# A hybrid FNet and mLSTM block in fp32: z and output gate of heads 1 to 3 as seven block products, x normalised early, u split in branch b

## The chip, the cores and the metric

The kernel runs on one core of a Trainium2 chip, in one launch. The metric is device time in microseconds (us). Before the change three runs took 775.4, 779.03 and 782.14 us; the median is 779.03. Line numbers (L88) are those of the kernel before, unless a sentence says "after".

## The reference

x is 512 positions by 1024 channels in fp32. All weights are fp32 too.

```python
h = rmsnorm(x, norm_w)
x_f, z_f, x_m, z_m, o_m, g_logits = split(h @ w_in)        # 1024, 1024, 2048, 2048, 2048, 2 x 1024 columns
y_a = (Re(fft2(x_f in 4 groups)) * silu(z_f)) @ w_fourier
x_c = silu(conv5(x_m)); q, k = block_diag(x_c); v = block_diag(x_m)
i, f gates of two directions = [q, k, v] @ w_gate + b
h_cell = mlstm(q, k, v, i, f) + flip(mlstm(flip(...)))       # 4 heads of 512 channels
h_cell = rmsnorm_per_head(h_cell * sigmoid(o_m)) * hnorm_w
y_b = ((h_cell + skip_w * x_c) * silu(z_m)) @ w_mlstm        # the bracket times silu(z_m) is u
x = x + (sigmoid(g_a) * y_a + sigmoid(g_b) * y_b) @ w_out
return rmsnorm(x, final_norm_w)
```

## The kernel before, in words

**fp32 products.** Each fp32 operand is split in two: hi, a rounded copy that ACT writes (`hi_of`, L85), and lo, the rest, that DVE subtracts (`lo_of`, L88). A product is three matmuls on TensorE (PE): hi hi, lo hi, hi lo (`mm3`, L95 to L97). The stationary tile is 128 x 128, the moving one 512 columns, or 256 in the block products.

**Weights.** They stream through `fetch` (L126, L129) on the DMA queue of SP, in units of 128 x 1024 (512 KB), into three `raw` buffers; `prepare` splits a unit into `whi` and `wlo`, `unit` hands it out. For the block products sums of weight blocks are needed: `sum_job` copies 1 MB from DRAM to DRAM on SP (L156) and adds 1 MB to it with an accumulating DMA that POOL issues (L160). One job runs at every third unit from unit 8 on, 17 in all. The accumulate of a job waits for the copy of the job before it.

**Order.** Work is written stage by stage, and a scheduler then sets the order of PE, ACT, DVE and POOL; instructions in `pin` keep the order of the text, as most weight transfers do. Each engine takes its instructions strictly in the order that results.

**Stages.** (1) x is loaded and split; its rows are squared and summed (`norm_rows`, L297): PE sums, DVE writes rc (L302), POOL takes the power -1/2 (L303). `norm_bcast` (L305) makes diagonals of rc on ACT (L308), multiplies them by a matrix of ones on PE (L310), and ACT writes rb (L311), the factor of each position. (2) 17 units of w_in give z of channel block 0 and x_m in 16 blocks (`proj`). They are made from x that is not normalised, and `evac` (L355) multiplies each by rb on DVE. Meanwhile the gate weights are folded with the block-diagonal q, k, v weights (`fold_gates`, L264: six multiplies on POOL, L273, and six reduces on DVE, L274); the convolution runs on DVE (L328) and feeds the gate matmuls. (3) Four heads. Each makes the scores (q by x_c), the decay weights, `o_unit` four times (L540: 24 matmuls of 512 columns each, x stationary) and `z_unit` four times (L366: 24 of 512, weights stationary), the denominators (L580 to L600; the reciprocal is L596), the split score weights whi and wlo in tiles phi and plo (L602 to L612), v (L618), the products pv (L633), the head norm (L634 to L640), transposes (L650) and u (L652, L653), which is split at once into tiles sa and sb. (4) Branch b: 16 units of w_mlstm times u, and beside it `block_sums` (L668), which loads x again, normalises it (L673) and makes the sums of its blocks, of which th, tl, bh and bl are the splits. (5) Sixteen `group`s: gates b, x_f, z_f, gates a. A group is a product of 2 x 2 blocks with seven block products in place of eight (Strassen-Winograd), each of 4 x 3 matmuls of 256 columns. X, Z and Y are its PSUM banks; sums in PSUM and on DVE (L725, L748, L754) put the blocks together. The Fourier stages run between them. (6) The product with w_fourier, the merge, w_out, residual and last norm.

PSUM has two kinds of banks, `acc` (4) and `wk` (4). Tiles named sa and sb, so0, so1, sz0, sz1 hold different things one after another; a tile is free when its last reader is done.

## Time and profile before

| | |
|---|---|
| median of three runs | 779.03 us (775.4 to 782.14) |
| the profiled execution | 782.93 us, of which the span of the trace is 781.0 |
| granted TensorE clock, mean | 0.995 |
| bytes moved by the DMA queues | 117.03 MB |

The profile is of one execution of its own. PE is TensorE's matmuls, PEld its weight loads, DVE VectorE, ACT ScalarE, POOL GpSimd, SP SyncE, "SPq" the DMA queue that SP fills. In a window's row each engine has its busy time and its count, then the clock, the DMA engines' busy share and GB/s. In a timeline row stand start, duration, engine, line, operation, output <- inputs, and in brackets the idle time before it and what ended that. A matmul's duration is longer than the step to the next one, as they overlap.

### The profile page before, as it was taken

Reading aid. Unit: us, or ns where it says so; the run is one execution under the profiler, and the core shown is the slowest. Engines: PE = TensorE matmul, PEld = TensorE weight load, DVE = VectorE, ACT = ScalarE, POOL = GpSimd, SP = SyncE. Lnnn points to the kernel's source line nnn. Section 1 sums busy time; section 2 is a strip of 40 time slices with the busy share of each in tenths; the row PEclk is TensorE's granted clock in tenths of the full one; section 3 lists DMA queues with packets and bytes.
Section 4 is the critical chain, followed back from the end, with each engine's and each line's share of the span. In section 5 each row is a group of like instructions: output and inputs, shape, how many; then the busy total and the mean of one; then the engine's idle time right before and its main releaser. Section 6 shows DMA issues by size and latency. Waiting matters only on the chain.

```text
span 781.0 us, 10974 instructions
## 1 busy us (share of the span) xinstructions
PE 766.3 (98%) x4182; PEld 654.9 (84%) x4182; DVE 525.0 (67%) x802; ACT 417.4 (53%) x658; POOL 67.2 (9%) x139
## 2 busy tenths in 40 slices
...
GB/s 300 235 141 209 214 179 92 28 161 138 80 189 102 167 109 162 42 174 154 197 27 162 141 257 90 105 193 217 190 161 159 121 166 192 144 144 169 172 55 55
DMA packets 39446, 117.03 MB, mean 150 GB/s; under 512 B 4577, under 2 KB 5090, under 8 KB 35298
## 3 DMA queue, kind: packets, MB, share of 16 engines
...
q14 instruction: 19, 0.16, 0.1%
HBM read 114.22 MB, written 35.65 MB: 192 GB/s over the span
## 4 chain that ended last, share of the span: by engine, by line
PE 93%; DVE 2%; DMA 2%; ACT 2%; issue 0%; SPq 0%; POOL 0%; POOLq 0%; ACTq 0%; DVEq 0%
PE acc L95 16%; PE acc L97 16%; PE acc L96 16%; PE wk L95 7%; PE wk L97 7%; PE wk L96 7%; PE acc L548 3%; PE acc L547 3%; PE acc L549 3%; PE wk L291 2%; PE acc L955 2%; PE acc L953 2%; PE acc L954 2%; PE wk L618 2%; DMA raw<-in_units_dram 2%; DVE wlo L88 1%
## 5 line engine op out<-in xcount | busy, mean ns | idle before, releaser
L88 DVE TENSOR_TENSOR wlo<-raw,whi 128x1024 fp32r<-128x1024 f32 (+1 forms) x103 | 128.4, 1249 | 84.0 <-ACT whi L85 83.9
L85 ACT ACTIVATE whi<-raw 128x1024 fp32r<-128x1024 f32 (+1 forms) x103 | 106.4, 1034 | 135.2 <-PE acc L96 98.0
L97 PE MATMUL acc<-hhi,wlo 128*128 128x512 f32 x248 | 97.3, 393 | 4.3 <-DVE wlo L88 4.3
L95 PE MATMUL acc<-hhi,whi 128*128 128x512 f32 x248 | 97.8, 397 | 0.8 <-ACT whi L85 0.8
L96 PE MATMUL acc<-hlo,whi 128*128 128x512 f32 x248 | 97.7, 394 | 0.0
L97 PEld LDWEIGHTS acc<-hhi,wlo 128*128 128x128 f32 x248 | 47.0, 190 | 15.5 <-DVE wlo L88 4.7
L95 PEld LDWEIGHTS acc<-hhi,whi 128*128 128x128 f32 x248 | 46.8, 189 | 11.6 <-ACT whi L85 1.2
L96 PEld LDWEIGHTS acc<-hlo,whi 128*128 128x128 f32 x248 | 47.0, 190 | 11.3 <-DVE hlo L199 0.7
L549 PE MATMUL acc<-whi,hlo 128*128 128x512 f32 x128 | 50.4, 394 | 0.0
L548 PE MATMUL acc<-wlo,hhi 128*128 128x512 f32 x128 | 50.4, 393 | 0.0
L96 PE MATMUL acc<-sb,whi 128*128 128x512 f32 x128 | 49.9, 391 | 0.0
L95 PE MATMUL acc<-sa,whi 128*128 128x512 f32 x128 | 49.8, 390 | 0.1
L96 PE MATMUL wk<-vlo,phi 128*128 128x512 f32 x128 | 49.8, 389 | 0.0
L95 PE MATMUL wk<-vhi,phi 128*128 128x512 f32 x128 | 49.8, 390 | 0.0
L97 PE MATMUL acc<-sa,wlo 128*128 128x512 f32 x128 | 48.6, 391 | 0.0
L97 PE MATMUL wk<-vhi,plo 128*128 128x512 f32 x128 | 48.0, 389 | 0.0
L547 PE MATMUL acc<-whi,hhi 128*128 128x512 f32 x128 | 47.7, 393 | 0.0
L328 DVE SCALAR_TENSOR_TENSOR t2k<-sa,vecs,t2k 128x511 f32<-128x511 f32 (+1 forms) x64 | 45.6, 739 | 0.0
L88 DVE TENSOR_TENSOR gwl<-raw,gwh 128x1024 fp32r<-128x1024 f32 x27 | 33.0, 1222 | 15.9 <-ACT gwh L85 15.9
L85 ACT ACTIVATE gwh<-raw 128x1024 fp32r<-128x1024 f32 x27 | 28.6, 1059 | 18.3 <-PE acc L96 8.3
L95 PEld LDWEIGHTS wk<-vhi,phi 128*128 128x128 f32 x128 | 24.0, 188 | 5.8 <-issue 0.8
L95 PEld LDWEIGHTS acc<-sa,whi 128*128 128x128 f32 x128 | 24.0, 188 | 5.4 <-ACT whi L85 0.5
...
## 6 DMA issues: line engine op xcount, KB each, us to landing
...
```

The costliest lines, as they stand in the source:

```text
L85: se.activation(dst, src, AF.Copy, scale=scale)
L88: ve.tensor_tensor(out=dst, in0=src, in1=hi.bitcast(F32), op=ALU.subtract)
L95: pin(te.matmul(acc, wh, xh, start=start, stop=False, **skip), pinned)
L96: te.matmul(acc, wh, xl, start=False, stop=False, **skip)
L97: te.matmul(acc, wl, xh, start=False, stop=stop, **skip)
L291: te.matmul(gate_ps, w_gate[j][:, i, :], r, start=p == 0 and n == 0, stop=last and n == 3)
L328: ve.scalar_tensor_tensor(out=cv[:, o], in0=src[:, s], scalar=cw[k], in1=cv[:, o], op0=ALU.mult, op1=ALU.add)
L547: te.matmul(ops[t], hv(x_hi, k)[:, ts], wh[:, ks], start=k == 0, stop=False)
L548: te.matmul(ops[t], hv(x_hi, k)[:, ts], wl[:, ks], start=False, stop=False)
L549: te.matmul(ops[t], hv(x_lo, k)[:, ts], wh[:, ks], start=False, stop=k == 7)
L618: te.matmul(vp[:, ds], xm[c0 + d][:, b * P : (b + 1) * P], vbf[:, d, :], start=True, stop=True)
L953: te.matmul(acc, m_hi[k][:, ts], wh, start=k == 0, stop=False)
```

## The change

**What it does.** (a) The z and o of heads 1 to 3 become block products of the class `Seven`. o takes 7 products of 24 matmuls of 256 columns (x parts stationary), z two groups of 7 products of 12 matmuls. Their block sums of weights join the jobs: `NB` is 7 instead of 4, 29 jobs instead of 17. Each of these heads now takes 14 units of 128 x 1024 instead of 8. Head 0 keeps the old form. (b) `scale_x` normalises x during units 3 to 5 (DVE, ACT, DVE) and writes it to DRAM; from unit 6 on `proj` uses it, and its outputs are copied by ACT instead of multiplied by rb on DVE. The block sums of x move to head 0 and read the normalised x back; the late ones go. (c) u stays in the tiles of x_c, and its split moves into branch b (`split_u`), to tiles sp0 to sp3 for the first four and to a pool "ub". (d) The fold's six multiplies run on DVE, in three steps at units 6 to 8. (e) The four acc banks become two px and two pz; a group's Z and Y use pz instead of wk. x_m of heads 2 and 3 goes through DRAM. In the heads, every third unit is split into sp tiles, and three split units instead of two are held ready.

**The early part on DVE.** Before, between the row sums and the second weight split (L302 is rc, L88 the lo of a weight unit or another split, L274 a reduce of the fold, L356 an evacuation by rb):

```order
L253 TENSOR_SCALAR m_45_215<-m_45_215 128x64
L302 TENSOR_SCALAR rc_222<-wk_301 128x4
L88 TENSOR_TENSOR wlo_289<-raw_184,whi_288 128x1024
L274 TENSOR_REDUCE sa_79_409<-sa_55_276 128x128
L274 TENSOR_REDUCE sa_79_409<-sa_56_278 128x128
L88 TENSOR_TENSOR wlo_332<-raw_187,whi_331 128x1024
L274 TENSOR_REDUCE sa_79_409<-sa_57_280 128x128
L356 TENSOR_TENSOR sz_51_248<-acc_223,rb_221 128x512
L356 TENSOR_TENSOR sa_54_275<-acc_250,rb_221 128x512
L356 TENSOR_TENSOR sa_66_330<-acc_294,rb_221 128x512
```

After, at the same place (L299 and L300 are the fold's multiply and reduce, L96 the lo, L332 is rc, L396 the evacuation, L380 `scale_x`):

```order
L96 TENSOR_TENSOR wlo_326<-raw_213,whi_325 128x1024
L300 TENSOR_REDUCE mhi_542<-tt_72_319 128x128
L299 TENSOR_TENSOR wf_74_323<-wf_74_323,vecs_127 128x512
L300 TENSOR_REDUCE mx_r_543<-wf_73_321 128x128
L96 TENSOR_TENSOR wlo_368<-raw_216,whi_367 128x1024
L332 TENSOR_SCALAR rc_251<-wk_338 128x4
L305 TENSOR_TENSOR mhi_542<-mhi_542 128x256
L300 TENSOR_REDUCE mx_r_543<-wf_74_323 128x128
L308 TENSOR_TENSOR wf_57_242<-mhi_542,wf_57_242 128x16x16
L308 TENSOR_TENSOR wf_58_243<-mx_r_543,wf_58_243 128x16x16
L396 TENSOR_TENSOR sz_65_285<-px_260,rb_250 128x512
L396 TENSOR_TENSOR sp_68_312<-pz_287,rb_250 128x512
...
L380 SCALAR_TENSOR_TENSOR vhi_6_128<-vhi_6_128,vecs_127,rb_250 128x512
```

The fold's multiplies and reduces and two weight splits stand ahead of rc, and the scaling of x stands between the evacuations and the convolution.

**The early part on SP.** Before (L262 gate weights, L156 the first copy for a sum, L126 weight units):

```order
L262 DMA sa_55_276<-in_gates_dram 128x512
L262 DMA sa_56_278<-in_gates_dram 128x512
L414 DMA gb_1259<-in_gbias_dram 64x2
L262 DMA sa_57_280<-in_gates_dram 128x512
L156 DMA sum_80<-in_blocks_dram 128x2048
L126 DMA raw_184<-in_units_dram 128x1024
L126 DMA raw_187<-in_units_dram 128x1024
L262 DMA sb_58_282<-in_gates_dram 128x512
L262 DMA sb_59_284<-in_gates_dram 128x512
L262 DMA sb_60_286<-in_gates_dram 128x512
L126 DMA raw_292<-in_units_dram 128x1024
```

After (L288 gate weights, L146 weight units, L182 the copy, L383 normalised x to DRAM):

```order
L288 DMA tt_71_317<-in_gates_dram 128x512
L288 DMA tt_72_319<-in_gates_dram 128x512
L288 DMA wf_73_321<-in_gates_dram 128x512
L146 DMA raw_213<-in_units_dram 128x1024
L146 DMA raw_216<-in_units_dram 128x1024
L288 DMA wf_74_323<-in_gates_dram 128x512
L146 DMA raw_329<-in_units_dram 128x1024
L466 DMA gb_1330<-in_gbias_dram 64x2
L182 DMA sum_83<-in_blocks_dram 128x2048
L146 DMA raw_371<-in_units_dram 128x1024
L383 DMA xn_256<-vhi_6_128 128x512
```

The copy moved behind three weight units and three more gate tiles.

**The start of branch b.** Before, on PE, the last product of the heads' z and the first of branch b (sa0 and sb0 are hi and lo of u's first block):

```order
L95 MATMUL acc_743_3652<-hhi3_17_125,whi_736_3612 128x512
L96 MATMUL acc_743_3652<-hlo3_21_129,whi_736_3612 128x512
L97 MATMUL acc_743_3652<-hhi3_17_125,wlo_737_3613 128x512
L95 MATMUL acc_776_3754<-sa0_350_1752,whi_740_3646 128x512
L96 MATMUL acc_776_3754<-sb0_351_1753,whi_740_3646 128x512
L97 MATMUL acc_776_3754<-sa0_350_1752,wlo_741_3647 128x512
L95 MATMUL acc_776_3754<-sa1_354_1764,whi_740_3646 128x512
```

After, on DVE, the end of head 3 and the first splits of u (L835 and L836 make u in the tiles of x_c, here sb12 to sb15; sp0 with an L96 row is the lo of u's first block, in tiles of two halves that ACT and DVE write):

```order
L607 SCALAR_TENSOR_TENSOR sz1_692_3715<-px_779_4236,sz1_692_3715 128x256
L835 SCALAR_TENSOR_TENSOR sb12_182_922<-wk_791_4370,vecs_5_127,sb12_182_922 128x512
L835 SCALAR_TENSOR_TENSOR sb13_188_939<-wk_792_4390,vecs_5_127,sb13_188_939 128x512
L835 SCALAR_TENSOR_TENSOR sb14_194_960<-wk_793_4397,vecs_5_127,sb14_194_960 128x512
L835 SCALAR_TENSOR_TENSOR sb15_198_979<-wk_794_4404,vecs_5_127,sb15_198_979 128x512
L836 TENSOR_TENSOR sb12_182_922<-sb12_182_922,sz0_691_3714 128x512
L836 TENSOR_TENSOR sb13_188_939<-sb13_188_939,sz0_691_3714 128x512
L836 TENSOR_TENSOR sb14_194_960<-sb14_194_960,sz1_692_3715 128x512
L96 TENSOR_TENSOR sp0_827_4450<-sb0_209_1043,sp0_827_4450 128x512
L836 TENSOR_TENSOR sb15_198_979<-sb15_198_979,sz1_692_3715 128x512
L96 TENSOR_TENSOR sp1_828_4456<-sb1_219_1095,sp1_828_4456 128x512
```

And on PE (px_779 is z's last block product, whose weights are in sp0 and sp1; pz_820 and px_821 are branch b's first two outputs):

```order
L103 MATMUL px_779_4236<-xph1_29_152,sp0_785_4287 128x256
L104 MATMUL px_779_4236<-xpl1_33_156,sp0_785_4287 128x256
L105 MATMUL px_779_4236<-xph1_29_152,sp1_786_4288 128x256
L103 MATMUL pz_820_4440<-sp0_827_4450,whi_788_4346 128x512
L103 MATMUL px_821_4441<-sp0_827_4450,whi_824_4444 128x512
L104 MATMUL pz_820_4440<-sp0_827_4450,whi_788_4346 128x512
L105 MATMUL pz_820_4440<-sp0_827_4450,wlo_789_4347 128x512
```

The splits of u's first blocks moved from head 0 to this place, behind the seven instructions that finish u in head 3, and into tiles that z's last product reads.

**The diff**, cut to what is spoken of (a late `group` is now a `Seven` in rows, with the same products in the same order):

```diff
 NRAW = 3
 NG = 16
+NB = 7
...
+SCALE_AT, NEW_AT, FOLD_AT = (3, 4, 5), 6, (6, 7, 8)
 Z_FIRST = 3
 LOW = ("ones", "mhalf", "warm", "vecs", "raw", "whi", "wlo", "consts", "rb", "rc", "rr", "ss", "fss", "gb")
...
+        if tag == "acc":
+            tag = ("px", "pz")[turns[0] % 2]
+            turns[0] += 1
+        return ps.tile([rows, cols], F32, tag=tag, name=f"{tag}_{count[0]}", bufs=4 if tag == "wk" else 2)
...
+    for b in range(3):
+        plan += [([blk(b, 0, 2 * S, name)], 8) for name in ("a11", "s1", "a12", "s2", "s4", "s3", "a22")]
+        seq = pairs_of([(b, 2 * S, 3 * S), (b, 3 * S, 4 * S)])
+        plan += [(seq[i : i + 2], 56) for i in range(0, len(seq), 2)]
...
+        tags, bufs = ("whi", "wlo"), 2
+        if N_HEAD0 <= i < N_HEADS and (i - N_HEAD0) % 3 == 2:
+            a = (0, 2, 0)[(i - N_HEAD0) // 14]
+            tags, bufs = (f"sp{a}", f"sp{a + 1}"), 1
+        elif first_pair <= i < last_pair and (i - first_pair) % 4 >= 2:
+            tags = ("gwh", "gwl")
...
         i = state["split"]
-        if i >= JOB_AT and (i - JOB_AT) % JOB_STEP == 0 and state["job"] < 17:
+        if i >= JOB_AT and (i - JOB_AT) % JOB_STEP == 0 and state["job"] < 4 * NB + 1:
             sum_job(state["job"])
             state["job"] += 1
-        while len(items) < (4 if "gw" in pools and state["split"] < last_pair else 2) and state["split"] < nplan - 8:
+        while len(items) < (4 if "gw" in pools and state["split"] < last_pair else 3 if N_HEAD0 <= state["split"] < N_HEADS else 2) and state["split"] < nplan - 8:
...
+        for n, t in enumerate(("tt4", "tt5", "tt6", "tt7", "wf2", "wf3")):
...
+        if not folds:
...
+        for half in range(2):
+            hs = slice(8 * half, 8 * half + 8)
+            g = grep[j, half]
+            w = wview(off)[:, hs].unsqueeze(2).to_broadcast([P, 8, 16, 4])
+            ve.tensor_tensor(out=g, in0=g, in1=w, op=ALU.mult)
+            ve.tensor_reduce(out=dst[:, hs, :], in_=g, axis=AX.X, op=ALU.add)
...
+        if i >= 8:
+            pin(nc.sync.dma_start(xm_out[i // 2][:, (i % 2) * S : (i % 2 + 1) * S], src))
...
+    def scale_x(k):
+        ve.scalar_tensor_tensor(out=xt[k], in0=xt[k], scalar=col(V_NW + k), in1=rb, op0=ALU.mult, op1=ALU.mult)
+        hi_of(x_hi[k], xt[k])
+        lo_of(x_lo[k], xt[k], x_hi[k])
+        pin(nc.sync.dma_start(xn_out[k % 4][:, (k // 4) * S : (k // 4 + 1) * S], xt[k]))
...
-        evac(sz[d], proj(), AF.Silu)
+        se.activation(sz[d], proj(x_hi, x_lo), AF.Silu)
...
-        acc = proj(hooks)
+        acc = proj(*((first_hi, first_lo) if n < NEW_AT else (x_hi, x_lo)), hooks)
...
+            if n >= NEW_AT:
+                se.activation(xm[i], acc, AF.Copy)
+                ready.append(i)
+            else:
+                waiting.append((i, xm[i], acc, None))
...
-        if n == FOLD_AT and not folded:
-            fold_gates()
+        if n in SCALE_AT:
+            at = SCALE_AT.index(n)
+            for k in range(3 * at, min(8, 3 * at + 3)):
+                scale_x(k)
+        if n in FOLD_AT:
+            fold_gates(FOLD_AT.index(n))
...
+    def block_sums(k):
+        xr = tl(f"sp{k % 2}", [P, 2, S])
+        nc.sync.dma_start(xr, xn_out[k].rearrange("p (a c) -> p a c", a=2))
...
+        def product(self, acc, name, first):
+            if self.rows:
+                wh, wl = block()
+                for k in range(4):
+                    ks = slice(k * P, (k + 1) * P)
+                    mm3(acc, wh[:, ks], wl[:, ks], xpart(0, name, k), xpart(1, name, k), first and k == 0, k == 3, group=False)
+                return
+            wh, wl = unit()
+            for k in range(4):
+                ks = slice(k * 256, (k + 1) * 256)
+                for t in range(2):
+                    ts = slice(t * P, (t + 1) * P)
+                    xh, xl = xpart(0, name, k)[:, ts], xpart(1, name, k)[:, ts]
+                    a = acc[:, t * 256 : (t + 1) * 256]
+                    go, end = first and k == 0 and t == 0, k == 3
+                    te.matmul(a, xh, wh[:, ks], start=go, stop=False, skip_group_check=True)
+                    te.matmul(a, xh, wl[:, ks], start=False, stop=False, skip_group_check=True)
+                    te.matmul(a, xl, wh[:, ks], start=False, stop=end, skip_group_check=True)
...
+        def p1(self):
+            self.X = self.new("px")
+            self.product(self.X, "b11", True)
+            se.activation(self.c11, self.view(self.X), AF.Copy)
+        def p5(self):
+            self.Z = self.new("pz")
+            self.product(self.Z, "t1", True)
+            se.activation(self.c22, self.view(self.Z), AF.Copy)
+        def p2(self):
+            Y = self.new("pz")
+            self.product(Y, "b21", True)
+            ve.tensor_tensor(out=self.c11, in0=self.view(Y), in1=self.c11, op=ALU.add)
...
+        def p6(self):
+            self.product(self.X, "t2", False)
+            se.activation(self.c12, self.view(self.X), AF.Copy)
...
+        def p3(self):
+            self.product(self.Z, "b22", False)
+            ve.tensor_tensor(out=self.c12, in0=self.view(self.Z), in1=self.c12, op=ALU.add)
...
+        def p7(self):
+            self.product(self.X, "t3", False)
+            ve.scalar_tensor_tensor(out=self.c22, in0=self.view(self.X), scalar=-1.0, in1=self.c22, op0=ALU.mult, op1=ALU.subtract)
...
+        def p4(self):
+            self.product(self.X, "t4", False)
+            se.activation(self.c21, self.view(self.X), self.func or AF.Copy, scale=-1.0)
...
-                bc = bank("acc")
+                bc = bank("acc" if h == 0 else "pz")
...
+        if h > 0:
+            o7 = Seven(so2[0][:, :, 0:256], so2[1][:, :, 0:256], so2[0][:, :, 256:512], so2[1][:, :, 256:512], False, None, AF.Sigmoid)
+            z7 = [seven_rows(sz[2 * n], sz[2 * n + 1], AF.Silu) for n in range(2)]
+            steps = [(o7.p1, o7.p5), (o7.p2, o7.p6), (o7.p3, o7.p7), (o7.p4,)]
...
+        if h >= 2:
+            for n in range(2):
+                both = tl(f"sp{2 * (h % 2) + n}", [P, 2, S])
+                nc.sync.dma_start(both, xm_out[2 * h + n].rearrange("p (a c) -> p a c", a=2))
+                xm[c0 + 2 * n], xm[c0 + 2 * n + 1] = both[:, 0], both[:, 1]
...
-        if h > 0:
-            z_unit(0)
+        if h == 0:
+            for k in range(4):
+                block_sums(k)
+        else:
+            for step in (z7[0].p1, z7[0].p5, z7[0].p2, z7[0].p6, z7[0].p3):
+                step()
...
+        if h > 0:
+            for step in (z7[1].p1, z7[0].p7, z7[1].p5, z7[1].p2, z7[1].p6, z7[0].p4, z7[1].p3, z7[1].p7):
+                step()
...
-            uu = t2k()
-            ve.scalar_tensor_tensor(out=uu, in0=tp, scalar=col(V_HN + c), in1=xc[c], op0=ALU.mult, op1=ALU.add)
-            ve.tensor_tensor(out=uu, in0=uu, in1=sz[d], op=ALU.mult)
-            u_hi[c] = tl(f"sa{c}", [P, S], F32R)
-            u_lo[c] = tl(f"sb{c}", [P, S], F32R)
-            hi_of(u_hi[c], uu)
-            lo_of(u_lo[c], uu, u_hi[c])
+            if h > 0 and d == 0:
+                z7[1].p4()
+            ve.scalar_tensor_tensor(out=xc[c], in0=tp, scalar=col(V_HN + c), in1=xc[c], op0=ALU.mult, op1=ALU.add)
+            ve.tensor_tensor(out=xc[c], in0=xc[c], in1=sz[d], op=ALU.mult)
...
+    def split_u(c):
+        if c < 4:
+            both = tl(f"sp{c}", [P, 2, S], F32R)
+            u_hi[c], u_lo[c] = both[:, 0], both[:, 1]
+        hi_of(u_hi[c], xc[c])
+        lo_of(u_lo[c], xc[c], u_hi[c])
...
                 j, c = (n, k) if n < 4 else (2 * (n % 2) + k // 4, 4 * (n // 2) + k % 4)
+                if c not in split:
+                    split.add(c)
+                    split_u(c)
                 ks = slice(k * P, (k + 1) * P)
                 mm3(accs[j], wh[:, ks], wl[:, ks], u_hi[c], u_lo[c], c == 0, c == 15)
```

330 lines of the change are left out of this document (166 added, 164 removed).

## The prediction

> **What bounds the kernel now.** The page's busy totals and its chain of waits come first, then single stretches.
>
> ```profile
> PE 766.3 (98%) x4182; PEld 654.9 (84%) x4182; DVE 525.0 (67%) x802; ACT 417.4 (53%) x658; POOL 67.2 (9%) x139
> PE 93%; DVE 2%; DMA 2%; ACT 2%; issue 0%; SPq 0%; POOL 0%; POOLq 0%; ACTq 0%; DVEq 0%
> 325.80:401.00 75.20, 75.20 (x357) 62.85 (x356) 50.69 (x84) 46.37 (x72) 10.57 (x20) 1.00 0.50 147
> ```
>
> TensorE is busy for 98% of the span and carries 93% of the chain. The third row is one stretch of 75.2 us, from the reciprocal of head 2 to that of head 3 (columns: PE, weight loads, DVE, ACT, POOL, clock, DMA share): PE never waits in it, DVE works 50.69 us, the DMA engines half of the time. So a product less is time less, as long as DVE and the DMAs, which the change loads more, stay under PE. The one large gap is early:
>
> ```profile
> 20.00:26.00 6.00, 6.00 (x35) 5.02 (x33) 0.80 (x2) 1.50 (x3) 2.75 (x3) 1.00 1.05 375
> 32.00:38.00 6.00, 5.24 (x16) 4.19 (x17) 6.00 (x10) 1.75 (x3) 0.00 (x0) 0.72 0.56 182
> 23.25 1.08 POOL L160 DMA_DIRECT2D sum<-in_blocks_dram  x1 [21.99 <-DMA sum<-in_blocks_dram]
> 24.17 1.36 POOL L303 TENSOR_TENSOR rc<-rc,mhalf 128x4 f32<-128x4 f32 x1
> 25.20 3.39 POOL L273 TENSOR_TENSOR sa<-sa,vecs 128x512 f32<-128x512 f32 x3
> 28.26 3.35 POOL L273 TENSOR_TENSOR sb<-sb,vecs 128x512 f32<-128x512 f32 x3
> 22.01 0.16 DVE L302 TENSOR_SCALAR rc<-wk 128x4 f32<-128x4 f32 x1 [2.05 <-PE wk L301]
> 25.36 7.35 DVE L88 TENSOR_TENSOR wlo<-raw,whi 128x1024 fp32r<-128x1024 f32 x1 [3.19 <-ACT whi L85]
> 33.82 1.21 DVE L88 TENSOR_TENSOR wlo<-raw,whi 128x1024 fp32r<-128x1024 f32 x1
> 26.89 1.13 PE L310 MATMUL wk<-sa,ones 128*128 128x512 f32 x2 [0.72 <-ACT sa L308]
> 32.76 0.58 PE L97 MATMUL acc<-hhi,wlo 128*128 128x512 f32 x1 [4.29 <-DVE wlo L88]
> 33.13 0.63 PE L95 MATMUL acc<-hhi,whi 128*128 128x512 f32 x1
> 33.56 0.63 PE L96 MATMUL acc<-hlo,whi 128*128 128x512 f32 x1
> ```
>
> A weight split (wlo) that takes 1.21 us elsewhere took 7.35 while POOL ran the six fold multiplies; PE stood 4.29 us for it. Then its matmuls start 0.43 us apart and the clock of that stretch reads 0.72: in 3.3 us (32.8 to 36.1) about 1.6 more are lost. The gap costs 0.72 + 4.29 + 1.6 = 6.6 us.
>
> **The products of heads 1 to 3.** Per head 192 matmuls of 512 columns become 336 of 256, with as many weight loads as matmuls.
>
> ```profile
> 480.00:500.00 20.00, 20.00 (x90) 16.55 (x89) 4.90 (x4) 3.38 (x4) 0.00 (x0) 1.00 0.29 93
> 540.00:560.00 20.00, 20.00 (x174) 20.00 (x173) 13.94 (x19) 12.04 (x20) 0.00 (x0) 1.00 0.63 203
> L95 PE MATMUL acc<-sa,whi 128*128 128x512 f32 x128 | 49.8, 390 | 0.1
> L95 PE MATMUL acc<-th,whi 128*128 128x256 f32 x100 | 28.1, 281 | 0.0
> ```
>
> The windows count every matmul that touches them, so the pitch is (20 + 0.39)/90 = 0.2266 us at 512 columns and (20 + 0.28)/174 = 0.1166 at 256. 192 x 0.2266 = 43.5, 336 x 0.1166 = 39.2: 4.3 less per head, **-13.0 us** for three. Bounds -12 and -14 from half a count. The margin is thin: at 43.5/336 = 0.1295 us per matmul nothing would be won, and in the second window the weight loads fill all 20 us.
>
> The Trainium skill (TensorE: Matmul & The Clock Gate, Back-to-back issue gap) speaks against such narrow products: it gives 131 ns per matmul at 512 columns and 81 at 128, on a straight line 98 at 256. By that ratio (an estimate) a head's products would take 336 x 0.098 = 32.9 instead of 192 x 0.131 = 25.2, 30% more. The two windows disagree, with 0.2266 and 0.1166 in this same program.
>
> **The early part.** The folds leave POOL, so the 7.35 us wlo goes. But two things move ahead of the norm. On SP the copy of the first sum now stands behind three weight units of 512 KB and three gate tiles of 256 KB that it preceded: 2.3 MB, at the 375 GB/s of the window from 20 us some 6.1 us. POOL's accumulate waits for that copy and the power that makes rc waits on POOL behind it, as at 23.25 and 24.17 above. So rc is done near 25.5 + 5.5 = 31. On DVE eleven fold instructions and two wlo now stand ahead of L332: 11 x 0.60 + 2 x 1.13 = 8.9 us from 20.0, where DVE ran out of work before, so about 28.9, the same date. Next late is the ones-matrix product of norm_bcast, on which PE queues unit 3:
>
> ```profile
> 25.56 1.28 ACT L308 ACTIVATE sa<-consts,rc 128x128 f32<-128x128 f32 x4 [0.23 <-POOL rc L303]
> 28.06 0.60 ACT L311 ACTIVATE rb<-wk 128x512 f32<-128x512 f32 x1 [0.27 <-PE wk L310]
> L673 DVE SCALAR_TENSOR_TENSOR xr<-xr,vecs,rb 128x512 f32<-128x512 f32 x8 | 5.9, 742 | 0.0
> ```
>
> 31 + 1.3 for the diagonals puts it at 32.4; PE, out of work at about 26.5, stands some 5 us, runs 1.6 slow, and has waited some 2 at the row sums before. Then DVE has the first evacuations, eight scalings (8 x 0.66 by the last row's shape, 0.74 less the 0.08 that neighbours overlap) and eight x splits (8 x 0.60) before the next wlo: I find two of them 1.3 and 0.7 late. 5 + 1.6 + 2 + 2 = 10.6 against 6.6: +4. If the copy lands as early as before, the gap shrinks to the 0.72 and the gain is -5; if both delays add, +6. I take **+2.5**: the order fixes the direction, the landing is the weak number. The 11 evacuations that leave DVE (11 x 0.60 = 6.6) pay for most of the other x work up to 135 us.
>
> **The heads' DVE chain.**
>
> ```profile
> L88 DVE TENSOR_TENSOR wlo<-raw,whi 128x1024 fp32r<-128x1024 f32 (+1 forms) x103 | 128.4, 1249 | 84.0 <-ACT whi L85 83.9
> L356 DVE TENSOR_TENSOR sz<-acc,rb 128x512 f32<-128x512 f32 x16 | 11.0, 686 | 10.9 <-PE acc L97 10.5
> L725 DVE SCALAR_TENSOR_TENSOR pr<-acc,p 128x256 f32<-128x256 f32 x8 | 3.3, 418 | 1.5 <-PE acc L97 1.5
> 323.07 0.69 DVE L595 TENSOR_TENSOR t2k<-t2k,phi 128x512 f32<-128x512 f32 x1
> 324.28 3.34 DVE L596 RECIPROCAL t2k<-t2k 128x512 f32<-128x512 f32 x1
> 341.18 0.82 DVE L88 TENSOR_TENSOR plo<-wf,phi 128x640 fp32r<-128x640 f32 x1
> 338.39 0.39 PE L95 MATMUL wk<-vhi,phi 128*128 128x512 f32 x1
> ```
>
> Per head, six more weight splits (14 for 8): 6 x 1.13 = 6.8. Block sums: three of 512 columns and six of 256, 3 x 0.61 + 6 x 0.34 = 3.9. Gone are four evacuations and four u splits, 8 x 0.60 = 4.8. So +5.9: about 57 us of DVE in a head of 75.2 - 4.3 = 70.9. The sum fits, but one chain decides: from the maximum (323.07) over the reciprocal to the last plo (342.0) 18.9 us, and the pv products wait at its end, PE reaching them at 338.39. Now four weight splits and about four sums fall into that chain (about 22 us), and the PE work beside it, o7's last products, v, and z7[0], lasts 20 to 21. I take 0.8 us of stall per head, **+2.5** in all; nothing is the lower bound (the rows of before show none), 4 per head the upper: **0 to +12**. Head 0's block sums (4 x 2.7 = 10.8 of DVE) lie under its 75 us of PE with 53 of DVE.
>
> **The start of branch b.** Before, u was split behind each head. Now the first u tiles sp0 and sp1 are also the weights of z7[1].p4, PE's last product ahead of branch b, and the lo of c = 0 stands on DVE behind four L835 and three L836.
>
> ```profile
> 436.08 2.06 DVE L652 SCALAR_TENSOR_TENSOR t2k<-wk,vecs,sb 128x512 f32<-128x512 f32 x3
> L653 DVE TENSOR_TENSOR t2k<-t2k,sz 128x512 f32<-128x512 f32 x16 | 10.3, 682 | 0.0
> L85 ACT ACTIVATE sa<-t2k 128x512 fp32r<-128x512 f32 x16 | 9.8, 629 | 18.7 <-DVE t2k L653 18.7
> 428.41 0.39 PE L97 MATMUL acc<-sa,wlo 128*128 128x512 f32 x1
> ```
>
> From the last transposes: 0.2 + 4 x 0.66 + 3 x 0.60 + 0.68 = 5.3 us until u_lo is there. PE has p4 (12 x 0.117 = 1.4, after 0.44 of transposes), waits 0.7 for the hi, has two products that need only it, and waits again: 5.3 - 0.44 - 1.4 - 0.45 = 3.0. Before, branch b began at 428.41 with no wait. **+3.0**; 1 if the transposes' sums run ahead of the row order, 5 if ACT's weight split stands before the hi.
>
> By the Trainium skill (TensorE: Matmul & The Clock Gate, What's actually happening) an idle window of about 3.4 us halves the clock for about as long; here 4.29 idle was followed by 0.43 us steps. By that rule a wait at this place beyond 3.4 would cost 1.7 more; 3.0 stays under it.
>
> **The rest.** The late groups lose two PSUM banks per role; an evacuation of 0.38 behind a 1.05 us split still lies under the 1.4 us of a product: **+0.5** (0 to +5). The later fnw load is covered by about 16 us of out products, at most 2 if not. x and xm through DRAM: 2 MB written, 2 MB read, no wait on the path. Branch b's DVE loses eight xr rows with their sums and gets sixteen u splits, in a stretch where PE waited 0.07: nothing.
>
> Sum: -13.0 + 2.5 + 2.5 + 3.0 + 0.5 = -4.5. The profiled execution took 782.93, so 778.4. It lies 3.9 above the median of 779.03; on that footing **774.5 us**. A measurement of this kernel tells 1% from no change: below 771.2 is faster, above 786.8 slower.
>
> **The rivals.** *Everything is covered* (0.27): the heads wait for nothing, as before, the copy lands early enough for the early part to come out even, branch b costs 1: -13.0 + 1 = -12, **767.0**. For it: 75.20 of 75.20 busy in the heads. Against: the rows on SP and POOL.
>
> *DVE takes over in the heads* (0.13): the plo chain ends 6 us after PE's cover in each of three heads, for instance when z7's sums are served before it. -4.5 + 18 - 2.5 = +11, **790**. It decides from 2.3 us per head for slower than before (7 us: 4.5 + 2.5), from 4.9 for more than 1%. For: the chain already ends 3.6 us after PE's first pv. Against: 14 us of DVE idle in each head.
>
> *The DMAs take over in the heads* (0.10):
>
> ```profile
> q1 hardware_dynamic: 3057, 13.77, 25.3%
> q0 software_dynamic: 864, 6.29, 22.2%
> ```
>
> In 150 us (250 to 400) q1 took 38.0 us for 13.77 MB, 2.76 per MB, and six accumulates 33.3, 5.55 each. A head of after moves 14 units (20.3), 4.67 copies (13.5), 4.67 accumulates (25.9) and xm (2): 62 of 70.9 us. If they run 25% longer when crowded, 77.5: +6.6 per head, 20 in all, less the chain's 2.5: **792**. It decides from 14% on. For: 44 to 50% of before becomes 87%. Against: three raw and three split buffers give each unit 14 us.
>
> *Weight loads bound the narrow products* (0.01): above 0.1295 us a head loses. At 0.14, 47.0 for 43.5: +10.6 instead of -13.0, **798**. Against: the 0.1166 of the same shape.
>
> **How the numbers follow.** The forecast has 0.49, with 768 to 783 as its own range, about a fifth of it below 771.2. Faster: 0.27 + 0.10 = 0.37. Slower: 0.18 of the three slower rivals, and 0.02 of the forecast where its bounds add, 0.20. Same: 0.43. The range leaves out the worst of the slower cases and the best of the covered one: 762 to 790.
>
> **What would show it.** Right: x336 fewer-column rows with 0.117 steps in the heads; L186 on POOL ahead of L333 released by the sum copy near 29; PE idle about 5 us before the ones product; a wait of PE on DVE sp1 of 2 to 4 us at the start of branch b; under 1.5 us of waits per head on plo. Wrong: PE waits on wlo or raw in the heads of over 5 us each, a DMA share above 0.95 there, or an early gap shorter than before.

## The result, and the profile after

The changed kernel takes 821.49 us (median of 4 runs, 818.82 to 824.62) where the kernel before took 780.59 on the same chip (4 runs, 775.4 to 782.26). The ratio is 1.0537, 95% interval 1.0466 to 1.0609: about 41 us slower. The forecast was 774.5, with 762 to 790 as its range; the prediction was wrong in sign and in size. Lines of this part and of the experiments are those of the kernel after (L93 is the hi of a split, L96 the lo, L103 to L105 the three matmuls, L146 the weight loads, L182 the copy of a sum job, L186 its accumulate); where a kernel is made from the one before, the text says so.

The page of after, its busy totals and its chain of waits:

```profile
PE 773.5 (95%) x4614; PEld 677.2 (83%) x4614; DVE 542.0 (66%) x839; ACT 449.7 (55%) x731; POOL 75.8 (9%) x145
PE 68%; DMA 10%; DVE 10%; ACT 7%; issue 3%; POOL 1%; SPq 0%; POOLq 0%; ACTq 0%; DVEq 0%
DMA packets 50829, 158.02 MB, mean 193 GB/s; under 512 B 5841, under 2 KB 6354, under 8 KB 43602
```

TensorE's share of the chain fell from 93% to 68%, and DMA, DVE and ACT now carry 27%. The totals hide this: PE still reads 95% busy, because a matmul's modelled duration is longer than the step to the next one. So the time was cut into stages. The work of a stage is its matmuls by width times the pitch of a full stretch (0.227 us at 512 columns, 0.117 at 256, 0.111 at 128), and its stall is the rest of the wall time, waits and slowed steps together; q and pv are the first products of a head's scores and of its weighted values, "b" is the start of branch b, "groups" that of the late groups, "f" the product with w_fourier. The table is worked out from the starts of all matmuls:

```
stall, us          before  after    e1    e2    e4    e6    e7   e10
start to q0          12.2   14.7  15.0  15.9  16.0  15.3  15.1  15.2
q0 to pv0             2.2    1.1   1.1   1.1   1.1   1.1   1.1   1.1
pv0 to q1             0.3    7.5   8.8  11.2   8.2  14.5   0.7   0.2
q to pv, heads 1-3    0.3    7.3   4.4   9.2   5.5   4.1   9.5   0.3
pv1 to q2             0.1    6.5   0.5   1.9   5.3   4.5   0.1   0.1
pv2 to q3             0.0    7.0   2.3   0.8   2.7   3.2   0.1   0.1
pv3 to b              0.0    6.9   5.0   4.2   4.1   4.2   0.7   0.1
b to groups           0.3    1.2   1.1   3.7   3.9   3.6   2.0   2.9
groups to f           2.8   15.5   2.7  15.0  21.4  11.8   3.1   2.3
f to the end          1.1    1.1   1.1   1.0   1.5   1.0   1.1   1.1
```

From before to after the stalls rise by 49.5 us. The work falls from 754.0 to 741.1, that is by 12.9. Together +36.6, and the spans differ by 817.5 - 781.0 = 36.5. The work is a count times a pitch, so its fall holds if the pitch holds in the new place; the heads of after show it (92 steps in a row from 248.04 us, 0.1168 each). Against it, four kinds of places lost 47 us: the heads 20.4 (q to pv, and behind pv1 and pv2), the end of head 0 7.2, the start of branch b 6.9, and the late groups, whose products the change leaves as they were, 12.7.

**The early part**, as windows of after (columns as before: PE, weight loads, DVE, ACT, POOL, clock, DMA share, GB/s) and rows of POOL, DVE and PE:

```profile
20.00:26.00 6.00, 4.81 (x25) 3.88 (x24) 6.00 (x11) 2.02 (x2) 0.00 (x0) 0.86 0.79 314
26.00:32.00 6.00, 4.39 (x14) 2.85 (x14) 4.03 (x8) 2.00 (x6) 2.23 (x2) 0.86 0.88 191
32.00:38.00 6.00, 6.00 (x28) 4.95 (x27) 5.26 (x9) 5.14 (x9) 0.00 (x0) 1.00 0.66 188
```

```profile
26.00 1.08 POOL L186 DMA_DIRECT2D sum<-in_blocks_dram  x1 [24.74 <-DMA sum<-in_blocks_dram]
28.43 1.16 POOL L333 TENSOR_TENSOR rc<-rc,mhalf 128x4 f32<-128x4 f32 x1 [1.34 <-DVE rc L332]
```

```profile
27.04 1.22 DVE L96 TENSOR_TENSOR wlo<-raw,whi 128x1024 fp32r<-128x1024 f32 x1
28.18 0.16 DVE L332 TENSOR_SCALAR rc<-wk 128x4 f32<-128x4 f32 x1
```

```profile
21.77 0.38 PE L331 MATMUL wk<-ones,plo 128*128 128x1 f32 x2 [1.19 <-DVE plo L271]
24.13 0.46 PE L103 MATMUL px<-sp,so 128*128 128x512 f32 x1
24.39 0.63 PE L104 MATMUL px<-sb,so 128*128 128x512 f32 x1
27.38 0.56 PE L105 MATMUL px<-sb,so 128*128 128x512 f32 x1
30.94 1.13 PE L340 MATMUL wk<-mlo,ones 128*128 128x512 f32 x2 [1.61 <-ACT mlo L338]
```

The 7.35 us split is gone (1.22 in its place), and rc comes at 28.2, held by the folds ahead of it on DVE, as forecast (28.9). The sum's copy, which was to land near 29, had landed by 26. PE lost little at the ones product, 1.61 in place of some 5: the product came at 30.9 and not 32.4, and PE had work until 29.3 and not 26.5, in part because it ran slow before: between 24.4 and 27.4 the steps are 0.43 us.

**Where the time went.** Windows of after in heads 1 and 2 and in the late groups:

```profile
260.00:280.00 20.00, 17.95 (x107) 15.36 (x107) 11.46 (x19) 11.67 (x24) 5.12 (x10) 1.00 1.02 318
280.00:300.00 20.00, 17.40 (x114) 15.38 (x113) 15.34 (x22) 18.35 (x28) 6.12 (x12) 1.00 1.01 241
320.00:340.00 20.00, 20.00 (x158) 19.19 (x157) 18.84 (x29) 16.03 (x24) 0.82 (x1) 1.00 0.95 264
540.00:560.00 20.00, 16.09 (x110) 15.48 (x108) 6.95 (x11) 7.89 (x13) 0.83 (x1) 0.83 0.98 278
560.00:580.00 20.00, 16.66 (x130) 15.66 (x131) 10.56 (x13) 8.37 (x13) 0.82 (x1) 1.00 0.90 263
```

In 540 to 560 the kernel before ran 174 matmuls at a DMA share of 0.63; after, 110 at 0.98, with DVE and ACT busy less than half of the time. That is the reading of a transfer limit: PE stands at times, the engines that feed it are idle half of the time, and the DMA engines are full. Part of that stall is slowed steps, as the granted clock there is 0.83. Now the chain at the end of head 1, and POOL's rows at that place (L819 and L820 make rr, the power of the head norm):

```profile
259.73 13.68 DMA sum<-in_blocks_dram
273.41 0.39 issue
273.80 0.81 POOL sum L186
274.96 0.56 POOL rr L820
```

```profile
273.80 0.81 POOL L186 DMA_DIRECT2D sum<-in_blocks_dram  x1 [12.90 <-DMA sum<-in_blocks_dram]
274.69 0.19 POOL L819 TENSOR_SCALAR rr<-ss 128x1 f32<-128x1 f32 x1
274.96 0.56 POOL L820 TENSOR_TENSOR rr<-rr,mhalf 128x1 f32<-128x1 f32 x1
```

The copy takes 13.68 us, where its median in the kernel before was 6.5. POOL stands 12.90 us at the accumulate, with the head norm queued behind it; ACT had the input of the norm's first step ready at 269.5 (L817), and POOL began it at 274.69. The wait it hands on is the largest in the list of PE's waits of after (released, total, times, longest; L832 are the transposes, L821 the scaling by rr):

```profile
PE wk L832 <- DVE so L821: 8.3, 5, 4.0
PE pz L103 <- ACT sz L588: 3.7, 2, 2.5
PE px L103 <- ACT whi L93: 2.7, 2, 2.2
PE px L103 <- DVE sz L607: 2.3, 1, 2.3
```

### The profile page after: what moved, and what is told of

It is laid out like the page before. It is cut to its first block, busy times and chain, and to the rows that moved or that the text cites. A ratio compares the mean times of both kernels' runs of the same rounds, so it can differ in the third digit from the quotient of the medians.

```text
span 817.5 us, 12146 instructions
## 1 busy us (share of the span) xinstructions
PE 773.5 (95%) x4614; PEld 677.2 (83%) x4614; DVE 542.0 (66%) x839; ACT 449.7 (55%) x731; POOL 75.8 (9%) x145
## 4 chain that ended last, share of the span: by engine, by line
PE 68%; DMA 10%; DVE 10%; ACT 7%; issue 3%; POOL 1%; SPq 0%; POOLq 0%; ACTq 0%; DVEq 0%
PE px L105 8%; PE px L103 8%; PE px L104 8%; PE pz L103 7%; PE pz L105 7%; PE pz L104 7%; DMA raw<-sum 5%; DMA sum<-in_blocks_dram 3%; PE wk L103 3%; PE wk L104 3%; PE wk L105 2%; DVE wlo L96 2%; PE wk L321 2%; ACT whi L93 1%; DMA raw<-in_blocks_dram 1%
## 5 line engine op out<-in xcount | busy, mean ns | idle before, releaser
L96 DVE TENSOR_TENSOR wlo<-raw,whi 128x1024 fp32r<-128x1024 f32 (+1 forms) x107 | 127.3, 1192 | 108.5 <-ACT whi L93 108.4
L93 ACT ACTIVATE whi<-raw 128x1024 fp32r<-128x1024 f32 (+1 forms) x107 | 110.5, 1035 | 145.8 <-PE px L104 77.4
L103 PE MATMUL pz<-xph,whi 128*128 128x256 f32 (+1 forms) x152 | 49.8, 328 | 3.7 <-ACT sz L588 3.7
L105 PE MATMUL px<-xph,wlo 128*128 128x256 f32 (+1 forms) x156 | 50.2, 322 | 1.2 <-DVE wlo L96 1.2
L103 PE MATMUL wk<-vhi,phi 128*128 128x512 f32 x128 | 49.9, 397 | 1.6 <-DVE vlo L96 1.6
L103 PE MATMUL px<-xph,whi 128*128 128x256 f32 (+1 forms) x156 | 50.5, 323 | 0.8 <-ACT whi L93 0.5
L104 PE MATMUL px<-xpl,whi 128*128 128x256 f32 (+1 forms) x156 | 50.2, 322 | 0.0
L105 PE MATMUL pz<-xph,wlo 128*128 128x256 f32 (+1 forms) x152 | 49.5, 326 | 0.5 <-DVE wlo L96 0.5
L104 PE MATMUL pz<-xpl,whi 128*128 128x256 f32 (+1 forms) x152 | 49.2, 323 | 0.0
L96 DVE TENSOR_TENSOR gwl<-raw,gwh 128x1024 fp32r<-128x1024 f32 x27 | 32.9, 1223 | 23.4 <-ACT gwh L93 23.3
L105 PE MATMUL wk<-vhi,plo 128*128 128x512 f32 x128 | 47.5, 390 | 0.0
L93 ACT ACTIVATE gwh<-raw 128x1024 fp32r<-128x1024 f32 x27 | 28.5, 1058 | 25.9 <-PE px L104 10.0
L103 PEld LDWEIGHTS pz<-xph,whi 128*128 128x128 f32 x152 | 29.1, 192 | 7.1 <-ACT sz L588 4.1
L105 PEld LDWEIGHTS px<-xph,wlo 128*128 128x128 f32 x156 | 29.7, 191 | 4.5 <-DVE wlo L96 1.8
L103 PEld LDWEIGHTS px<-xph,whi 128*128 128x128 f32 x156 | 29.9, 192 | 3.8 <-ACT whi L93 0.9
L105 PEld LDWEIGHTS pz<-xph,wlo 128*128 128x128 f32 x152 | 29.1, 191 | 3.9 <-DVE wlo L96 1.0
L104 PEld LDWEIGHTS px<-xpl,whi 128*128 128x128 f32 x156 | 29.8, 191 | 2.3
L186 POOL DMA_DIRECT2D sum<-in_blocks_dram x14 | 12.1, 864 | 208.8 <-DMA sum<-in_blocks_dram 208.5
L103 PE MATMUL px<-tt,whi 128*128 128x256 f32 x100 | 29.0, 290 | 2.2 <-ACT whi L93 2.2
L103 PEld LDWEIGHTS wk<-vhi,phi 128*128 128x128 f32 x128 | 24.5, 191 | 7.4 <-DVE vlo L96 1.8
```

Source lines behind the costliest of these rows:

```text
L93: se.activation(dst, src, AF.Copy, scale=scale)
L96: ve.tensor_tensor(out=dst, in0=src, in1=hi.bitcast(F32), op=ALU.subtract)
L103: pin(te.matmul(acc, wh, xh, start=start, stop=False, **skip), pinned)
L104: te.matmul(acc, wh, xl, start=False, stop=False, **skip)
L105: te.matmul(acc, wl, xh, start=False, stop=stop, **skip)
L186: gp.dma_start(sums[b, k], src, accum_op=ALU.add, max_dma_last_dim=4 * S * 4)
```

## The experiments

The theories at this point: JOBS, that the twelve added sum jobs (1 MB copied, 1 MB accumulated each) fill the DMA engines just when the narrow products ask for weights fastest; QUEUE, that it is less the bytes than the accumulate that blocks POOL ahead of the head norm; and that DVE or ACT are the late ones. The kernel before was timed again beside each experiment; its median there lies between 781.6 and 782.9.

**e1: no sum jobs.** Weights are read from the unsummed blocks, in pieces of the same size.

```diff
-            return sums[b, int(name[1]) - 1][:, c0:c1]
+            return blocks[b, int(name[1]) - 1][:, c0:c1]
...
-        if i >= JOB_AT and (i - JOB_AT) % JOB_STEP == 0 and state["job"] < 4 * NB + 1:
+        if i >= JOB_AT and (i - JOB_AT) % JOB_STEP == 0 and state["job"] < 0:
```

> The changed kernel without its 29 sum jobs: no copy and no accumulate is issued, and where a block sum of weights was read a plain block of the same size is read, so the block products use other numbers than the reference's; every transfer to SBUF, every split and every matmul stays. Three theories for the 41 us between the forecast direction and the result (821.5 against 780.6). JOBS: the twelve added sum jobs cost it, by filling the DMA engines and by their accumulates holding POOL's queue, on which the head norm's power stands; then nearly all stalls of the heads, of the start of the late groups and part of branch b's start go: 68.9 us of PE stalls fall to 25 to 32, the time to 776 to 786. CHAIN: DVE and ACT are too loaded in the heads (their chains end behind PE); then the stalls of the heads stay: 805 to 822. BANKS: two px and two pz banks in place of four make the block products wait for their evacuations; then heads and late groups stay as they are: 810 to 822.

Measured: 791.86 us (791.31 to 793.97), ratio to before 1.015 (1.0095 to 1.0206). The windows of e1 at the places shown above:

```profile
260.00:280.00 20.00, 20.00 (x126) 17.95 (x125) 15.70 (x26) 15.02 (x29) 3.69 (x8) 1.00 0.47 158
540.00:560.00 20.00, 20.00 (x173) 20.00 (x173) 13.14 (x17) 11.64 (x20) 0.00 (x0) 1.00 0.55 184
```

The jobs cost 821.5 - 791.9 = 29.6 us (27.0 between the two profiled spans, 817.5 and 790.5), and the late groups are whole again (15.5 to 2.7 us of stall). But 791.9 is above what JOBS alone allowed: 9 to 10 us over the kernel before remain, though 12.9 of work are gone. Something else costs over 20 us. The table says where: end of head 0 (8.8), start of branch b (5.0), q to pv (4.4).

**e2: accumulate later.** Each accumulate is issued one job later, when its copy should have landed, and POOL's order is pinned so that the head norm isn't behind it.

```diff
-        if i > 0:
-            b, k = (i - 1) // 4, (i - 1) % 4
+        if i > 1:
+            b, k = (i - 2) // 4, (i - 2) % 4
...
-            gp.dma_start(sums[b, k], src, accum_op=ALU.add, max_dma_last_dim=4 * S * 4)
+            pin(gp.dma_start(sums[b, k], src, accum_op=ALU.add, max_dma_last_dim=4 * S * 4))
...
```

> All jobs as in the changed kernel, with the same bytes, but each accumulate is issued two jobs behind its copy instead of one, and POOL's accumulates and head norm steps keep the order of the text. Its copy has then landed long before, so POOL does not wait in front of the power of the head norm. JOBS has two parts. If POOL's queue is the one that counts (the accumulates at 273.8, 357.2 and 428.9 us waited 12.9, 7.8 and 12.7 us with the power behind them), the stalls between the pv products and the next head's scores (7.0 and 6.5 us, and 6.9 before branch b) fall to 1 to 2 each: 803 to 811. If the filled DMA engines count alone, it stays at 817 to 824. CHAIN and BANKS: 817 to 824.

Measured: 813.19 us (809.92 to 816.58), ratio 1.0419 (1.0354 to 1.0484). POOL's rows of e2 at the end of head 1 (the first and the last of them):

```profile
274.78 0.19 POOL L819 TENSOR_SCALAR rr<-ss 128x1 f32<-128x1 f32 x1 [42.27 <-ACT t2k L817]
...
280.79 1.05 POOL L186 DMA_DIRECT2D sum<-in_blocks_dram  x1
```

The head norm now goes ahead of the accumulate and waits for its own input only. The stalls behind pv1, pv2 and pv3 fall from 20.4 to 6.9 together, so the block on POOL is real. But other stalls rise by 9 (the start, the end of head 0, q to pv, branch b), and the late groups stay at 15.0. The time lies between what the two parts of JOBS allowed. The span is 4.8 us shorter than in the changed kernel: the same bytes, moved a little, stand in the way at the next place.

**e3: the copies on another queue.** They are issued from ACT's queue, so that weight loads don't stand behind them on SP's.

```diff
-            pin(nc.sync.dma_start(sums[i // 4, i % 4], blocks[i // 4, (2, 0, 0, 1)[i % 4]], max_dma_last_dim=4 * S * 4))
+            pin(nc.scalar.dma_start(sums[i // 4, i % 4], blocks[i // 4, (2, 0, 0, 1)[i % 4]], max_dma_last_dim=4 * S * 4))
```

> The 28 copies of the sum jobs are issued from ACT's DMA queue instead of SP's; bytes and accumulates stay. If weight units were late because they stand behind a 1 MB copy in SP's queue, the waits on raw go (about 2.3, 2.1 and 2 us near 545 to 570 and 5 us before the pv of head 3): 808 to 815. If the 16 DMA engines themselves are full there, units and copies share them as before: 817 to 825, and worse where ACT holds the issue of a copy back. CHAIN and BANKS: no change, 817 to 824.

Measured: 830.9 us (825.82 to 831.53), ratio 1.0624 (1.0548 to 1.07): worse than the change as it is. The waits of ACT for weights, in e3:

```profile
ACT whi L93 <- DMA raw<-sum: 23.0, 8, 8.4
ACT gwh L93 <- DMA raw<-sum: 12.5, 3, 11.0
```

In the changed kernel the same two rows read 8.0 and 7.9. Only the loads of sums are waited for longer: for those of plain blocks the same two tiles wait 11.9 us, against 12.6 in the changed kernel. A copy itself lands no later (7.5 us against 8.0, medians). Why the sums come late is not shown; the copies now take their turn among ACT's instructions, and that may hold them back. So this run shows only that taking the copies out of SP's queue does not help.

**e4: the jobs spread.** From unit 44 on a job comes at every fourth unit instead of every third.

```diff
-        if i >= JOB_AT and (i - JOB_AT) % JOB_STEP == 0 and state["job"] < 4 * NB + 1:
+        if (i >= JOB_AT and (i - JOB_AT) % JOB_STEP == 0 if i <= 44 else (i - 44) % 4 == 0) and state["job"] < 4 * NB + 1:
```

> From unit 44 on a sum job runs at every fourth unit instead of every third, so that the jobs end near unit 108 instead of 92; the number of jobs and their bytes stay. If the filled DMA engines cost the time, heads 2 and 3, branch b's start and the start of the late groups get a quarter less of jobs: 5 to 12 us faster, 809 to 816. If POOL's queue counts, about the same stalls at other places: 815 to 824. CHAIN and BANKS: 819 to 824.

Measured: 819.9 us (813.03 to 820.63), ratio 1.0485 (1.0415 to 1.0555), above the 809 to 816 expected for full DMA engines and inside the 815 to 824 for POOL's queue. The stalls behind pv1 to pv3 fall from 20.4 to 12.1, those of the late groups rise from 15.5 to 21.4, with the jobs running on to about 625 us. What is taken from one place turns up at the next.

**e5: twelve more jobs in the kernel before.** Nothing else is changed: it does 29 jobs instead of 17, of which the last twelve make sums that nobody reads.

```diff
...
-        if i < 16:
+        if i < 28:
...
-        if i >= JOB_AT and (i - JOB_AT) % JOB_STEP == 0 and state["job"] < 17:
+        if i >= JOB_AT and (i - JOB_AT) % JOB_STEP == 0 and state["job"] < 29:
```

> The kernel before with twelve more sum jobs (29 in place of 17) at the same pace of one job per three units; the added ones write sums that nothing reads. PE's work is that of before. With 29 jobs the pace goes on from unit 59 to unit 92, so the last nine or ten stand among the late groups, where a unit of two blocks lasts 24 x 0.117 = 2.8 us on PE, three units 8.4, while the DMA engines need 3 x 1.55 + 8.45 = 13.1 us for three units and a job; the ones before stand where a unit lasts 5.4 us (three: 16.3) and the same 13.1 fit. JOBS in this form (bursts: a job hurts where units are used up fast): no stalls added up to the late groups, there 3 to 4.5 us per job, 25 to 40 in all: 800 to 820. If it were the average load of the DMA engines (65% of the span at most), or what a job does to POOL: 780 to 788.

Measured: 813.22 us (809.65 to 820.16), ratio 1.0435 (1.0359 to 1.051). The twelve added copies are issued from 455 us on, so the heads get none of them. Four fall into branch b, whose products of 512 columns don't notice them (0.3 us of stall, as before); the other eight fall among the groups, whose stall goes from 2.8 to 36.1. First e5's windows, then the longest pieces of its chain there (L85 is the hi):

```profile
520.00:540.00 20.00, 14.88 (x96) 13.98 (x96) 8.07 (x10) 6.89 (x11) 1.62 (x2) 0.83 0.99 307
540.00:560.00 20.00, 13.77 (x92) 12.87 (x92) 7.71 (x10) 7.23 (x12) 0.84 (x1) 0.83 1.01 270
560.00:580.00 20.00, 15.45 (x115) 14.64 (x114) 9.03 (x11) 7.98 (x13) 1.63 (x2) 0.94 1.03 300
```

```profile
526.58 15.74 DMA raw<-in_blocks_dram
542.37 0.05 issue
542.42 1.06 ACT whi L85
```

For the late groups this is the cleanest run on the cause: with none of the changed products, added jobs cost 32 us (813.2 against 781.6), all of it where 256-column products run. Nobody reads the added sums, so no load waits for one of them to be made. Half of a weight unit, 256 KB, takes 15.74 us in the chain. For the heads the evidence is e1.

**e6: the jobs in the pauses.** 18 of the 29 jobs are issued at chosen units, the others between the products of heads, where PE works on scores and pv, and POOL's order is pinned as in e2.

```diff
+JOB_CALLS = (6, 9, 11, 14, 16, 19, 21, 66, 68, 71, 73, 76, 78, 84, 92, 100, 108, 116)
...
+        if state["call"] in JOB_CALLS:
+            job()
+        state["call"] += 1
...
```

> The changed kernel with all 29 jobs, but none at units of heads 1 to 3: seven at units 6 to 21, three per head at its start, ahead of pv and ahead of the transposes, where PE uses up no units, six in branch b and five in the late groups, eight units apart. Accumulates and the head norm's steps on POOL keep the order of the text. JOBS by bursts: the stalls of heads 1 to 3 fall from 27 to 10 or less and those of the late groups from 15.5 to 6 or less: 795 to 806. If the sheer amount of DMA work counts, it only moves: 815 to 824. CHAIN and BANKS: 815 to 824.

Measured: 813.68 us (808.56 to 813.89), ratio 1.0408 (1.0335 to 1.0481): above what was expected. The late groups improve to 11.8 and the stalls behind pv1 to pv3 to 11.9, but the end of head 0 goes to 14.5. No timing of 29 jobs that was tried has a median below 813 us.

**e7: no jobs, no block sums of x, u split early.** On e1: the products read four plain blocks of x, so the 4 x 12 sums and splits of head 0 go, and the first four blocks of u are split in head 3, ahead of the instructions that finish its own u, into tiles that z's last product does not read.

```diff
-            for k in range(4):
-                block_sums(k)
+            pass
...
                 z7[1].p4()
+                if h == 3:
+                    for n in range(4):
+                        split_u(n)
...
```

> As the run without jobs (791.9 us; block sums of weights replaced by plain blocks), and besides: the block sums of x in head 0 are left out (plain blocks of x stand for them in the products), and u of blocks 0 to 3 is split before the transposes of head 3, into tiles that z's last product does not read. What the run without jobs still lost against before is 8.5 us after pv of head 0, 5.0 at the start of branch b, 2.8 early and some 6 in heads 2 and 3. If DVE's block sums hold back the head norm of head 0, that stall goes from 8.8 to 1 or less; if the late split of u makes branch b wait, its 5.0 go to 2 or less: 778 to 783 together. If PSUM banks or the chains of the heads make these waits (BANKS, CHAIN), both stay: 788 to 793.

Measured: 783.61 us (782.38 to 787.9, 10 runs), ratio 1.0048 (1.0015 to 1.008). The two stalls go as expected, 8.8 to 0.7 and 5.0 to 0.7. For e1 against e7 that is 8.3 us of time. The window of after at the end of head 0 showed who was full there (third figure, DVE, 19.59 of 20):

```profile
200.00:220.00 20.00, 16.67 (x97) 14.31 (x96) 19.59 (x40) 16.06 (x35) 6.32 (x10) 0.83 0.74 216
```

And the change still gains nothing: 9.5 us now stand between q and pv of heads 1 to 3, up from 4.4; that the other stalls had covered this work before is likely and not shown.

**e8: the fold alone, in the kernel before.** Part (d) by itself.

```diff
-                pin(gp.tensor_tensor(out=g, in0=g, in1=w, op=ALU.mult))
+                ve.tensor_tensor(out=g, in0=g, in1=w, op=ALU.mult)
```

> The kernel before, with one edit: the six multiplies of the gate fold run on VectorE instead of GpSimd (part d of the change alone, at its old place in the program). FOLD theory (the 7.35 us weight split was slow because GpSimd multiplied beside it, and PE's 4.29 us wait with its slow steps followed from that): the split takes about 1.2 to 2 us, PE's wait before 33 us is under 2, the stall before the first q product falls from 12.2 to 6 to 9, and the time is 3 to 6 us under the kernel before (ratio 0.992 to 0.996). Rival ROOM: six multiplies of 0.6 us more on VectorE push the rc or the split back by as much, and the wait stays 3 us or more; the ratio is 0.997 to 1.002. In the changed kernel this part could not be read by itself, because the scaling of x and a later copy came with it.

Measured: 778.82 us (777.79 to 780.62, 12 runs), ratio 0.9978 (0.9958 to 0.9998). The rows of DVE in e8, and its window beside the 0.72 of before:

```profile
25.44 0.15 DVE L302 TENSOR_SCALAR rc<-wk 128x4 f32<-128x4 f32 x1
25.51 1.22 DVE L88 TENSOR_TENSOR wlo<-raw,whi 128x1024 fp32r<-128x1024 f32 x1
```

```profile
32.00:38.00 6.00, 6.00 (x28) 4.94 (x28) 6.00 (x13) 3.98 (x8) 0.00 (x0) 1.00 0.35 144
```

The mechanism is that of FOLD: the split takes 1.22 us, the 4.29 us wait and the slow steps are gone. The size is between the two: the stall before q0 falls by 3.1 us, since rc comes 3.4 us later than before, and the time by 0.2%, some 2 us. Of the kernels here that leave nothing out it is the only one that is not slower than the kernel before, and by little: the runs of before beside it spread from 775.27 to 783.93.

**e9: evacuations on VectorE.** On e7: the copies of p1, p5 and p6 of the heads run on DVE.

```diff
-            se.activation(self.c11, self.view(self.X), AF.Copy)
+            self.out(self.c11, self.X)
...
+                ve.tensor_copy(out=dst, in_=self.view(acc))
...
```

> The kernel of e7 (no sum jobs, no block sums of x, u split early; the products read the wrong blocks, so the output is not the reference's) with the copies out of PSUM after p1, p5 and p6 of the heads on VectorE instead of ScalarE. Question: whose lateness makes the 9.5 us of stall between the first q and the first pv products of heads 1 to 3 (2.6, 3.4, 3.5 in e7; 0.1 each before). Theory ACT: ScalarE is full there with weight splits, three table loads, and the copies, in the order of its queue, and PE's rows name the copies L598 and L589; with nine copies per head away the three stalls together fall below 5 us and the time is 3 to 6 us under e7 (777 to 781 against 783.6). Rival DVE: VectorE carries the softmax chain in the same stretch and becomes the late one; stalls stay at 8 to 12 and the time is within 2 us of e7. Rival BANKS: the two px and two pz banks are the limit whoever copies; stalls stay at 8 to 11.

Measured: 783.85 us (783.1 to 785.02, 10 runs), ratio 1.0039 (1.0012 to 1.0066), as e7; q to pv 8.5 for 9.5. The theory that ACT is late through these copies falls. The names in PE's waits only change from ACT's copies to DVE's sums and splits, so two theories stay: too few banks, or too much work on both engines.

**e10: half of each split.** On e7: the weight units of heads 1 to 3 are split in half of their columns, and each product takes its first two blocks twice. Matmuls, banks, evacuations and transfers are as many as in e7.

```diff
+        if N_HEAD0 <= i < N_HEADS:
+            if len(plan[i][0]) == 1:
+                vh, vl, vr = (t[:, 0:512] for t in (hi, lo, r))
+            else:
+                vh, vl, vr = (t[:, 0:1024].rearrange("p (a c) -> p a c", a=2)[:, :, 0:256] for t in (hi, lo, r))
...
+                kw = k % 2 if self.head else k
...
```

> The kernel of e7 (no sum jobs, no block sums of x, u split early) in which each of the 42 weight units of heads 1 to 3 has only half of its columns split, and each product takes its first two weight blocks twice. The matmuls, evacuations, banks and transfers are the same in number; ScalarE and VectorE have 42 x about 0.5 us and 42 x 0.6 us less to do. The output is not the reference's. Question: after e9, what makes the 9.5 us of stall between q and pv of heads 1 to 3. Theory SPLITS: a narrow product lasts 2.8 us a unit, and ScalarE and VectorE must split a unit (1.05 and 1.22 us), evacuate it and run the softmax chain in that time; with half of the split gone the three stalls fall from 9.5 to 2 to 5 and the time is 4 to 8 us under e7 (776 to 780). Rival BANKS: two px and two pz banks with accumulations that wait for the evacuation of the bank; stalls stay at 7 to 11, time 781 to 785. Rival CHAIN: the waits come from the order in which the softmax and the table loads stand in the queues; stalls 5 to 8, time 779 to 782.

Measured: 775.86 us (773.71 to 776.86, 10 runs), ratio 0.9925 (0.9895 to 0.9955). Head 2 from q to pv, in e7 and then in e10:

```profile
294.10:334.40 40.30, 37.81 (x269) 35.03 (x268) 31.45 (x55) 25.09 (x39) 0.00 (x0) 1.00 0.32 106
```

```profile
281.70:316.90 35.20, 35.20 (x254) 33.03 (x253) 25.66 (x49) 19.87 (x32) 0.00 (x0) 1.00 0.27 92
```

The three stalls go from 9.5 to 0.3. With as many banks and evacuations nothing waits there, so the banks alone are not the limit: BANKS falls, and SPLITS stands: PE takes a unit of narrow products in 24 x 0.117 = 2.8 us, while DVE's split takes 1.2 of it and ACT's 1.05, with the softmax, the sums and the evacuations of the same products beside them. On average it fits (DVE 31.45 of 40.30), in the bursts it doesn't.

## Why the prediction was wrong

The runs in a row take the loss apart: 821.5 as changed; 791.9 without the jobs (29.6 us); 783.6 also without the block sums of x and the late split of u (8.3); 775.9 with half of the weight splits of the heads (7.8). Only at 775.9 does the gain of the products show (0.9925 of the kernel before), in a kernel that leaves out the sums and half of the splits which the change needs.

*Products: right.* -13.0 was forecast, the work fell by 12.9. The pitch of 0.117 holds in the changed kernel too: in its heads (0.1168, as above), in e10, where q to pv loses 0.3 us in three heads at that pitch, and in the late groups, 174 matmuls in 20 us, with the weight loads at 20.00:

```profile
660.00:680.00 20.00, 20.00 (x174) 20.00 (x173) 15.44 (x24) 15.50 (x31) 0.00 (x0) 1.00 0.48 145
```

The Trainium skill's ratio of narrow to wide matmuls (TensorE: Matmul & The Clock Gate, Back-to-back issue gap) would, by an estimate from its figures, have made the products a loss; the traces show 0.227 and 0.117 us instead. The weight-load rival falls too.

*Early part: right in size by luck.* Forecast +2.5, and the stall before q0 rose by 2.5, but by other steps. The date of rc was right through DVE and wrong through POOL: at 26.0 the copy was down, 2.75 us later than before (23.25), where I had charged 6.1 for the loads ahead of it. The gap at the ones product was 1.61 and not 5, the slow stretch came before it and not after. And the 6.6 us of gap that I let go were not all to be had: e8, with the fold alone, got 3.1.

*DMAs in the heads: the first wrong step.* The rival was priced as "62 of 70.9 us" per head, an average over a head in which units come evenly. They don't come evenly: 14 units of 2.8 us are 39 us of the 70.9. A burst of three units asks the DMA engines for 3 x 1.45 = 4.4 us of loads and one job of 2.9 + 5.5 = 8.4, together 12.8, in 3 x 2.8 = 8.4 us of PE. The same three rows gave this sum; I divided by the wrong time. "Three raw and three split buffers give each unit 14 us" was the second half of the error: at 2.8 us a unit, three buffers give 8.4. The sum thus put the transfers at nothing in the heads, where the stalls from q to pv and behind pv1 and pv2 fall by 13.6 us together once the jobs are gone (e1). The sign that I had named for this rival, a DMA share above 0.95, stands in the windows from 260 to 300 (1.02 and 1.01); its chance was 0.10 and its price 792, as it priced the heads alone.

*Late groups: the term that was missing.* They had "+0.5" for two PSUM banks, and no word on the jobs that now run beside them. 29 jobs at every third unit from unit 8 reach unit 8 + 28 x 3 = 92, and the groups start at unit 82 (66 of the heads and before, 16 of branch b), here at 536 us. POOL's row of after for the last accumulate:

```profile
567.62 0.82 POOL L186 DMA_DIRECT2D sum<-sum  x1 [14.21 <-DMA sum<-in_blocks_dram]
```

The banks cost nothing there: e1 has the same ones and 2.7 us of stall, as before. With the jobs the stall rose by 12.7, and in e5 by 33 in the old kernel. The quoted window at 540 us with its DMA share of 0.63 was the warning: a job of 8.4 us more per 8.4 us of PE can't fit beside it.

*POOL's queue.* I named the accumulate that stands ahead of a power on POOL in the early part, where it came out harmless, and not in the heads, where the same two instructions stand, four per head. There it cost what e2 gave back behind pv1 to pv3, 13.5 us of stall, though not of time.

*Block sums of x in head 0.* "Lie under its 75 us of PE with 53 of DVE" again divided by the whole head. They stand together behind pv0, where DVE then reads 19.59 of 20 and the head norm waits its turn: 7.2 us more stall at that place.

*Branch b: right in kind, short in size.* Forecast 3.0 with 5 as the bound; 6.9 as changed and 5.0 without the jobs, and 0.7 once u is split early (e7). The wait that I described, for the hi and the lo of u, is the smaller part: 0.6 and 0.8 us in PE's waits. What was not in the sum is that the last products of z wait as well. The PE rows of after:

```profile
441.10 0.66 PE L832 MATMUL wk<-consts,so 128*128 128x128 f32 x4 [0.74 <-DVE so L821]
444.03 0.50 PE L103 MATMUL px<-xph,sp 128*128 128x256 f32 x1 [2.28 <-DVE sz L607]
```

*Chain of the heads.* +2.5 was forecast for a late plo; q to pv rose by 7.0 as changed, by 9.2 in e7. The chain is not what PE waits for: in head 2 it takes 18.9 us before, 19.0 after and 19.5 in e7, and no wait of PE on a head's plo stands in the list of after or of e7. As changed, 5.4 of the 7.3 us stand in head 3, behind a late load of a sum:

```profile
400.08 9.83 DMA raw<-sum
410.01 1.06 ACT sp L93
411.10 1.24 DVE sp L96
```

Without the jobs it is the splits in the burst of products ahead of the chain's end (e10).

Not settled: whether jobs half as large or a smaller share of products (o alone, z as before) would leave a gain; neither was tried. Nor is it shown why before's groups bear 0.63 to 0.71 of DMA share with 2.8 us of stall, and from 0.9 on lose so much; the runs show the two ends only.
